# Order of the wide and narrow products inside the feed-forward panels: four orders in turn instead of one

## The chip, the cores and the metric

The kernel runs on one core of a Trainium2 chip. The metric is the device time of one execution in microseconds; three runs of the kernel before gave 3351.51 us (median), 3348.92 us (lowest) and 3356.8 us (highest). Lower is better.

## The reference

Three transformer-like blocks run one after another on 256 tokens of 2048 features, in fp32. Blocks 2 and 3 end in a feed-forward part, and these two parts are what the change touches:

```python
D_MODEL, SEQ, D_FF = 2048, 256, 8192
# block 2, and block 3 with w_up, w_down in place of w_ff1, w_ff2
h = rms_norm(x, g)
x = x + jnp.square(jax.nn.relu(h @ w_ff1)) @ w_ff2      # 2048 -> 8192 -> 2048
```

Everything else (a recurrence, three kinds of attention, gating, pooling) is computed around them by background tasks and stays as it is.

## The kernel before, in words

Every weight product of the kernel runs through one function, `run` (line 180), over a list of `Panel`s. A panel is 512 columns of a weight times an activation of 256 tokens, over `nk` = 16 blocks of 128 rows. The panel is cut into 4 **groups** of 4 row blocks (`kg` = 4), and a group into 4 **units** `j`, one for each 128 output features. Each unit of a panel has a PSUM bank of its own (tags m0 to m3); a unit's sum grows over the four groups.

To keep fp32 accuracy a weight is split in two: `whi` is the rounded part, `wlo` the rest. The activation is stored as (hi | lo) next to each other, 512 columns. So each row block of a unit needs two products: a **wide** one (line 249: `whi` times all 512 columns) and a **narrow** one (line 250: `wlo` times the 256 hi columns, added into the right half of the bank). A unit in a group is thus 4 wide and 4 narrow products, a group 16 pairs, a panel 64 pairs. Each product loads its own 128x128 weights first (PEld in the profile), and the load runs beside the product before.

```python
mm(out, hi[:, c], a, start=st, stop=False, skip_group_check=True)
mm(out[:, 256:512], lo[:, c], a[:, 0:256], start=False, stop=en, skip_group_check=True)
```

While group i is multiplied, the weights of group i+1 are split by `cut`: ScalarE casts `wf` to `whi` (line 209), VectorE subtracts to get `wlo` (line 210), once for each half of a group (two row blocks). `cut` for the first half is written behind unit 0 of group i, for the second half behind unit 1. There are 4 buffers of `whi` and of `wlo`, that is two groups.

After the last group of a panel each unit is taken out of its bank by `sum_halves`: ScalarE copies the right half (line 272), VectorE adds the left half to it (line 275), and the bank is free for the same unit of the next panel. Written order on the engines at the end of a panel is therefore: copy of unit 0, cast of half 0, copy of unit 1, cast of half 1 on ScalarE; `wlo` of half 0, add of unit 0, `wlo` of half 1, add of unit 1 on VectorE. Both engines work strictly in that order. What follows an add differs: in the first product of the feed-forward (an **up** panel) relu, square and a split into `hid` (lines 1101, 1103, 280, 282), in the second (a **down** panel) a multiplication and an addition to `x` on VectorE (lines 1114, 1116).

`ff` (line 1086) writes the panels of a feed-forward part: for each of 4 slices `d` of 2048 hidden features, four up panels `q` = 0 to 3 and four down panels `q` = 0 to 3. That makes 32 panels in each of the two parts, 64 in all, 4096 pairs. The other panels that matter below are those of mode "T" (lines 255 to 257), in which all three products of a row block are 512 wide.

Of the kernel before, what the change touches and what calls it, by code (L numbers as in the profile page):

```python
# [17 lines left out]
# columns of the packed per-feature vectors (each vector of n features takes n / 128 columns)  # L18
# [15 lines left out]
class Panel:  # L34
    """Products of one block of weight columns with an activation held as (hi | lo) tiles.
    w: the weight as it is loaded, [block of columns, unit of rows, 128, rows / 128 * columns]."""

    def __init__(self, w, c0, ncols, nk, act, evac, mode="F", k0=0, pre=None, post=None, load=None):
        self.w, self.c0, self.ncols, self.nk, self.act, self.evac = w, c0, ncols, nk, act, evac
        self.mode, self.k0, self.pre, self.post, self.load = mode, k0, pre, post, load  # L40
        self.kg = min(nk, 2048 // ncols)
        self.ngroups = nk // self.kg
        self.half = self.kg // 2


class FM:
    """A feature-major tensor [128 * n, 256] as tiles of four rows of blocks."""
# [8 lines left out]
class HL:  # L56
    """An activation (hi | lo), two blocks of 128 features to a tile."""
# [8 lines left out]
class Builder:  # L66
# [64 lines left out]
    def step(self, busy=False):  # L131
        """One stage of each task; of the evacuations' later stages only a few, none in a busy slot."""
# [24 lines left out]
    def wait(self, key):  # L157
        """st[key], in a task: other tasks go on until it is there."""
        while key not in self.st:
            yield  # L160
        return self.st[key]

    def wait_tiles(self, *keys, n=4):
        """The n products of each of the keys, in a task."""
        for key in keys:
            for j in range(n):
                yield from self.wait((key, j))

    def get(self, key, f):
        """Block f of the (hi | lo) activation st[key], once it is on its way."""  # L170
        self.require(lambda: key in self.st and f in self.st[key].ready)
        return self.st[key][f]

    def start(self, gen):
        """First stage of what happens to a product; the further ones follow, one a step."""
# [4 lines left out]
    def run(self, panels):  # L180
# [39 lines left out]
        for i, (p, g) in enumerate(groups):  # L220
# [12 lines left out]
            # where, among the units of this group, the next group is split  # L233
            when = (0, 1) if len(units) == 4 else (-1, 0 if len(units) == 2 else -1)
            for u in range(2):
                if when[u] < 0:
                    cut(i + 1, u)
            for j, tag in units:
# [3 lines left out]
                for kk in range(p.kg):  # L242
                    hi, lo = hs[kk // p.half][:, kk % p.half, :], ls[kk // p.half][:, kk % p.half, :]
                    a = p.act(g * p.kg + kk)
                    st = g == 0 and kk == 0
                    en = last and kk == p.kg - 1
                    if p.mode == "F":
                        c = slice(j * 128, (j + 1) * 128)
                        mm(out, hi[:, c], a, start=st, stop=False, skip_group_check=True)  # L249
                        mm(out[:, 256:512], lo[:, c], a[:, 0:256], start=False, stop=en, skip_group_check=True)  # L250
                    else:
                        ah = a[:, j * 128:(j + 1) * 128]
# [5 lines left out]
                self.step(j in when)  # L258
                if last:
                    self.start(p.evac(j, out))  # L260
                if j in when:
                    cut(i + 1, when.index(j))
                if p.mode == "T":
                    self.step()
# [3 lines left out]
    def sum_halves(self, p):  # L268
        """The product of a weight tile: its two halves in PSUM, added."""
# [8 lines left out]
    def split_act(self, dst, src):  # L278
        """dst (hi | lo) of src, both parts exact."""
# [4 lines left out]
    def scaled_split(self, dst, src, g):  # L284
        """dst (hi | lo) of src * g, g one number per partition."""
# [10 lines left out]
    def sum_sq(self, accs):  # L296
        """Sums over partitions and tiles ([128, 256] each), token-major, in PSUM [128, 2]."""
# [15 lines left out]
    def bcast_psum(self, rt):  # L313
        """A token-major [128, 2], over all partitions: [128, 256]."""
# [12 lines left out]
    def attention(self, heads, q, k, v, bias, dim, out):  # L327
        """Softmax attention of query tiles (tokens 0-127 on keys 0-127, 128-255 on 0-255).
        q, k: feature-major [dim, 256]; v(h, t): token-major [128, dim]; bias(h, s, p) is a task that
        writes s [128, 384] = scores + bias; out(i, psum [128, 256])."""  # L330
# [49 lines left out]
    def block1_constants(self):  # L380
# [19 lines left out]
        # 1 - x of mu_r, mu_k, mu_v and of k_a  # L400
# [5 lines left out]
    def input_norm(self, x, gname, hl, key):  # L406
        """hl (hi | lo) of x * g, four blocks at a time, then st[key]: sums of squares."""
# [17 lines left out]
    def load_x(self, name, between=False):  # L425
        """x, feature-major; the later tiles between the first tiles of the weights, or at once."""
# [10 lines left out]
    def block1(self):  # L437
# [36 lines left out]
        # attention, eight heads at a time: q, k feature-major, v token-major  # L474
# [44 lines left out]
        # LoRA: (h + (shift(h) - h) mu) w = h ((1 - mu) w) + shift(h) (mu w)  # L519
# [23 lines left out]
        def mixed(key, n, hf):  # L543
            """y + (shift(y) - y) mu of the product y"""
# [25 lines left out]
        # gated attention branch  # L570
# [70 lines left out]
        # merged branches  # L641
# [59 lines left out]
    def residual(self, hl, gname, key):  # L701
        """x += rms(o) post_norm_g; hl of x * g for what follows; st[key] of 1 / rms(x)."""
# [24 lines left out]
    def rwkv(self, hf):  # L727
        """The recurrence of eight heads, in chunks of 64 tokens."""
# [4 lines left out]
        # decay and in-context rate  # L733
# [16 lines left out]
        # 1 / max(|k k_k|, 1e-12) per head  # L750
# [72 lines left out]
        # (I - L)^-1 per head and chunk: diagonal blocks of 32 by substitution, one block per partition  # L823
# [58 lines left out]
        # the block below the diagonal: X21^T = X11^T L21^T X22^T  # L882
# [19 lines left out]
        # the recurrence over chunks  # L902
# [31 lines left out]
        # par: heads 2i + par; features, and tokens of V, at f; tokens of U at w  # L934
# [53 lines left out]
        # per token and head normalised y stands in v, feature-major  # L988
# [18 lines left out]
    def group_norm(self, y, out, key):  # L1007
        """Per token and head (over 64 values): (y - mean) / sqrt(var + eps), turned feature-major.
        y: PSUM [128, 4, 64], heads 2i on the lower tokens, 2i + 1 on the upper."""
# [27 lines left out]
    def rstd_task(self, key, sums, n, scale=None, square=False):  # L1037
        """st[key] = (token-major, over partitions, over partitions * scale or squared) of 1 / rms."""
# [19 lines left out]
    def acc_sq(self, accs, x, i, n, scale=None, last=1):  # L1058
        """accs, whose sum is the sum of the n tiles (x * scale)^2: the last ones stand by themselves."""
# [26 lines left out]
    def ff(self, w1, w2, h, rkey, done):  # L1086
        """x += relu(norm(x) w1)^2 w2, 2048 hidden features at a time; done(f) when x[f] is whole.
        h is x g: the square of 1 / rms(x), one number a token, comes in after w2."""
# [37 lines left out]
        for d in range(4):  # L1126
            for q in range(4):
                P.append(Panel(w1, 2048 * d + 512 * q, 512, 16, lambda kt: self.get(h, kt), up(d, q)))
            for q in range(4):
                P.append(Panel(w2, 512 * q, 512, 16, lambda kt, d=d: hact(d, kt), down(d, q), k0=16 * d))  # L1130
        return P

# [10 lines left out]
    def block2(self, start):  # L1143
# [20 lines left out]
        # index scores and the 64 keys of each query  # L1164
# [48 lines left out]
        # spatial gating: v token-major  # L1213
# [87 lines left out]
    def topk(self):  # L1301
# [35 lines left out]
        for t in range(2):  # L1337
# [12 lines left out]
            # 0 for a key that is selected and not after its query, else large and negative  # L1350
# [5 lines left out]
    def mixing(self):  # L1356
        """Layer norm of gelu(v) over features, and its causal mix over each 128 tokens."""
# [72 lines left out]
    def two_norms(self):  # L1430
        """x = rms(x) final_g (r1), then the scale of rms of that (r2); st["r3"] is r1 r2."""
# [127 lines left out]
    def pool(self, hf):  # L1559
        """Trailing means minus the value, two groups of 256 channels, mixed within each group."""  # L1560
# [94 lines left out]
def _dilated_bias():  # L1655
    """-slope * distance + ln(number of patterns that hold the key); far below where none does."""
# [8 lines left out]
def _tiles(w, cols=512, rows=256):  # L1665
    """A weight [K, C] in blocks of columns, each in units of rows that stand as they are loaded."""
# [5 lines left out]
def host_layout(i):  # L1672
    """The inputs as the program reads them: slices, transposes and gathers only; and constants
    of the shapes."""
# [46 lines left out]
```

## Time and profile before

| what | value |
|---|---|
| median of three runs | 3351.51 us |
| span of the profiled execution, first to last instruction | 3342.3 us |
| TensorE (PE) busy | 3288.9 us, 98% of the span |
| weight loads (PEld) busy | 2826.5 us, 85% |
| VectorE (DVE) busy | 2066.9 us, 62% |
| ScalarE (ACT) busy | 1716.4 us, 51% |
| share of the DMA engines | about 0.6 in the feed-forward parts |
| feed-forward of block 2, from about | 1604 to 2315 us |
| feed-forward of block 3, from about | 2617 to 3327 us |

The execution that was profiled has no time of its own apart from its span; the median stands 9.2 us above the span, and a change of the span is carried over to the median as it is. Durations of products in the profile overlap (their ends are modelled), so the pace of TensorE is read from the distance of starts, not from the durations.

### The profile page before, as it was taken

To read this page: it belongs to the slowest core of one execution; us is meant where nothing else is said; L and a number is where in the kernel's file an instruction comes from. 1 tells how busy PE (TensorE), PEld (TensorE's weight loads), DVE (VectorE), ACT (ScalarE), POOL (GpSimd) and SP (SyncE) were. 2 spreads that over 40 slices of the span, in tenths; PEclk is the share of its full clock that TensorE was granted. 3 is DMA by queue.
4 is the path that set the end of the run, shared out by engine and by line. 5 is a ranking of instruction groups with operands and counts; after the bars stand their busy time and mean duration, and the time that the engine had idled before them with its cause. 6 is when DMAs were issued, how large, how long until landed. Compare 5 with 4: busy or idle time off the path is not lost.

```text
span 3342.3 us, 50547 instructions
## 1 busy us (share of the span) xinstructions
PE 3288.9 (98%) x19438; PEld 2826.5 (85%) x19438; DVE 2066.9 (62%) x3034; ACT 1716.4 (51%) x2868; POOL 556.2 (17%) x568
## 2 busy tenths in 40 slices
PE   8999999999989999999999999999999999999998
PEld 7787888888878888888888888888888888888887
DVE  5577657646476546576555555658757755565556
ACT  5454544435444574455545545456455654545454
POOL 2132131204130322233100000004224300000001
PEclk9999999999989999999999999999999999999999
DMA  6555535535545555656565556565555556655564
GB/s 205 167 160 162 158 95 170 164 120 188 190 131 172 184 156 183 196 184 187 184 200 189 185 188 196 189 189 184 183 178 166 184 185 188 195 189 189 188 191 145
DMA packets 175585, 589.91 MB, mean 177 GB/s; under 512 B 28784, under 2 KB 31984, under 8 KB 175344
## 3 DMA queue, kind: packets, MB, share of 16 engines
q1 hardware_dynamic: 174624, 585.47, 55.8%
q8 instruction: 152, 2.49, 0.3%
q10 hardware_dynamic: 720, 1.22, 0.1%
q14 instruction: 89, 0.73, 0.1%
HBM read 582.95 MB, written 3.67 MB: 176 GB/s over the span
## 4 chain that ended last, share of the span: by engine, by line
PE 76%; DVE 4%; issue 3%; ACT 2%; POOL 1%; DVEq 0%; POOLq 0%; ACTq 0%
PE pm L249 45%; PE pm L250 23%; DVE wlo L210 2%; PE pm L255 1%; PE pm L257 1%; PE pm L256 1%; ACT whi L209 1%; DVE ev L275 0%; PE ppv L365 0%; POOL ev L661 0%; PE pgr L912 0%; PE psc L338 0%; PE pY L978 0%; PE ppl L1591 0%; DVE mr L1344 0%
## 5 line engine op out<-in xcount | busy, mean ns | idle before, releaser
L210 DVE TENSOR_TENSOR wlo<-wf,whi 128x1024 fp32r<-128x1024 f32 x1086 | 1349.4, 1266 | 1128.6 <-ACT whi L209 1109.2
L249 PE MATMUL pm<-h,whi 128*128 128x512 f32 x3872 | 1376.0, 398 | 12.9 <-ACT whi L209 8.7
L209 ACT CAST whi<-wf 128x1024 fp32r<-128x1024 f32 x1086 | 1107.2, 1050 | 479.8 <-PE pm L249 391.3
L250 PE MATMUL pm<-h,wlo 128*128 128x256 f32 x3872 | 1087.9, 281 | 6.7 <-DVE wlo L210 6.6
L249 PEld LDWEIGHTS pm<-h,whi 128*128 128x128 f32 x3872 | 727.0, 188 | 188.9 <-ACT whi L209 9.0
L250 PEld LDWEIGHTS pm<-h,wlo 128*128 128x128 f32 x3872 | 733.3, 189 | 12.1 <-DVE wlo L210 11.5
L249 PE MATMUL pm<-hid,whi 128*128 128x512 f32 x2048 | 710.8, 391 | 0.0
L250 PE MATMUL pm<-hid,wlo 128*128 128x256 f32 x2048 | 573.3, 280 | 0.0
L272 ACT COPY ev<-pm 128x256 f32<-128x256 f32 x491 | 181.2, 369 | 695.5 <-PE pm L250 679.8
L249 PEld LDWEIGHTS pm<-hid,whi 128*128 128x128 f32 x2048 | 383.1, 187 | 84.6
L249 PE MATMUL pm<-hb,whi 128*128 128x512 f32 x1168 | 421.0, 403 | 11.4 <-DVE hb L717 8.6
L250 PEld LDWEIGHTS pm<-hid,wlo 128*128 128x128 f32 x2048 | 387.0, 189 | 0.0
L1072 POOL TENSOR_TENSOR acc<-acc,sqa 128x256 f32<-128x256 f32 x104 | 120.2, 1162 | 1496.0 <-ACT sqa L1067 1472.5
L250 PE MATMUL pm<-hb,wlo 128*128 128x256 f32 x1168 | 330.1, 283 | 1.3 <-DVE wlo L210 1.1
L249 PEld LDWEIGHTS pm<-hb,whi 128*128 128x128 f32 x1168 | 221.4, 190 | 68.3 <-issue 8.7
L250 PEld LDWEIGHTS pm<-hb,wlo 128*128 128x128 f32 x1168 | 223.4, 191 | 4.2 <-DVE wlo L210 3.1
L275 DVE TENSOR_TENSOR ev<-pm,ev 128x256 f32<-128x256 f32 x491 | 198.9, 416 | 27.0 <-ACT ev L272 26.8
L249 PE MATMUL pm<-mg,whi 128*128 128x512 f32 x512 | 179.6, 395 | 0.0
L250 PE MATMUL pm<-mg,wlo 128*128 128x256 f32 x512 | 143.8, 281 | 1.0 <-DVE wlo L210 1.0
L249 PEld LDWEIGHTS pm<-mg,whi 128*128 128x128 f32 x512 | 96.0, 187 | 22.6
L250 PEld LDWEIGHTS pm<-mg,wlo 128*128 128x128 f32 x512 | 96.7, 189 | 1.7 <-DVE wlo L210 1.6
L255 PE MATMUL pm<-whi,hb 128*128 128x512 f32 x160 | 66.0, 412 | 0.0
(353 smaller groups left out, 3099.9 us busy)
## 6 DMA issues: line engine op xcount, KB each, us to landing
wf<-w_in SPq DMA_DIRECT2D x312, 512.0 KB, 4.0
wf<-w_ff SPq DMA_DIRECT2D x256, 512.0 KB, 4.4
wf<-w_sgu SPq DMA_DIRECT2D x128, 512.0 KB, 3.9
wf<-w_up SPq DMA_DIRECT2D x128, 512.0 KB, 4.4
wf<-w_down SPq DMA_DIRECT2D x128, 512.0 KB, 4.3
wf<-w_out SPq DMA_DIRECT2D x96, 512.0 KB, 4.3
wf<-w_branch_attn SPq DMA_DIRECT2D x16, 512.0 KB, 3.6
wf<-w_branch_rwkv SPq DMA_DIRECT2D x16, 512.0 KB, 4.1
```

What stands on the lines that cost most here:

```text
L209: self.nc.scalar.copy(hi, t)
L210: self.nc.vector.tensor_tensor(lo, t, hi.bitcast(F32), op=ALU.subtract)
L249: mm(out, hi[:, c], a, start=st, stop=False, skip_group_check=True)
L250: mm(out[:, 256:512], lo[:, c], a[:, 0:256], start=False, stop=en, skip_group_check=True)
L255: mm(o, ah, hi, start=st, stop=False, skip_group_check=True)
L256: mm(o, ah, lo, start=False, stop=False, skip_group_check=True)
L257: mm(o, al, hi, start=False, stop=en, skip_group_check=True)
L272: nc.scalar.copy(a, p[:, 256:512])
L275: nc.vector.tensor_tensor(b, p[:, 0:256], a, op=ALU.add)
L1072: nc.gpsimd.tensor_tensor(accs[0], accs[0], s, op=ALU.add)
```

## The change

Each panel gets an `order`, 0 to 3, and `ff` gives panel `q` the order `q`, for up and down panels alike. All other panels keep order 0, which is the order before: wide, narrow, wide, narrow. Order 1 takes two row blocks at a time: two wide, then two narrow products. Order 2 takes the whole group: four wide, then four narrow. Order 3 takes two units together: for each row block the wide product of unit j-1 and of unit j, then the narrow ones of both; evacuation and `cut` of both units come behind the second. The rest of the diff removes comments and docstrings, which moves line numbers (209 becomes 210, 249 becomes 247 in "F" mode, 275 becomes 310).

```diff
+            def products(j, half):
+                ...
+                    if kind == "h":
+                        mm(out, hs[kk // p.half][:, kk % p.half, c], a, start=g == 0 and kk == 0, stop=False,
+                           skip_group_check=True)
+                    else:
+                        mm(out[:, 256:512], ls[kk // p.half][:, kk % p.half, c], a[:, 0:256], start=False,
+                           stop=last and kk == p.kg - 1, skip_group_check=True)
+
+            def after(j):
+                self.step(j in when)
+                if last:
+                    self.start(p.evac(j, ps[j]))
+                if j in when:
+                    cut(i + 1, when.index(j))
...
+                    if p.order == 3 and len(units) == 4:
+                        if j % 2 == 0:
+                            if g == 0:
+                                ps[j + 1] = self.pm.tile([128, 512], F32, name="pm", tag=units[j + 1][1])
+                            continue
+                        for kk in ks:
+                            for kind in "hl":
+                                for jj in (j - 1, j):
+                                    products(jj, [(kind, kk)])
+                        after(j - 1)
+                        after(j)
+                        continue
+                    if p.order == 1:
+                        seq = [(kind, kk + d) for kk in range(0, p.kg, 2) for kind in "hl" for d in range(2)]
+                    elif p.order == 2:
+                        seq = [(kind, kk) for kind in "hl" for kk in ks]
                     else:
+                        seq = [(kind, kk) for kk in ks for kind in "hl"]
+                    products(j, seq)
...
-                P.append(Panel(w1, 2048 * d + 512 * q, 512, 16, lambda kt: self.get(h, kt), up(d, q)))
+                P.append(Panel(w1, 2048 * d + 512 * q, 512, 16, lambda kt: self.get(h, kt), up(d, q), order=q))
...
-                P.append(Panel(w2, 512 * q, 512, 16, lambda kt, d=d: hact(d, kt), down(d, q), k0=16 * d))
+                P.append(Panel(w2, 512 * q, 512, 16, lambda kt, d=d: hact(d, kt), down(d, q), k0=16 * d, order=q))
```

**On TensorE, the start of up panel 3 (order 3) in slice d = 0 of block 2's part.** `pm_15990` is the bank of unit 0; the bank of unit 1 is `pm_16005` before and `pm_15992` now; `pm_15817` is the bank of the panel before. Before:

```order
L250 MATMUL pm_15817<-h2_15305,wlo_15903 128x256
L249 MATMUL pm_15990<-h2_14620,whi_15937 128x512
L250 MATMUL pm_15990<-h2_14620,wlo_15938 128x256
...
L250 MATMUL pm_15990<-h2_14652,wlo_15954 128x256
L249 MATMUL pm_16005<-h2_14620,whi_15937 128x512
L250 MATMUL pm_16005<-h2_14620,wlo_15938 128x256
```

and now:

```order
L250 MATMUL pm_15817<-h2_15305,wlo_15903 128x256 x2
L247 MATMUL pm_15990<-h2_14620,whi_15937 128x512
L247 MATMUL pm_15992<-h2_14620,whi_15937 128x512
L250 MATMUL pm_15990<-h2_14620,wlo_15938 128x256
L250 MATMUL pm_15992<-h2_14620,wlo_15938 128x256
...
L247 MATMUL pm_15990<-h2_14652,whi_15953 128x512
L247 MATMUL pm_15992<-h2_14652,whi_15953 128x512
```

The first product into the bank of unit 1 stood ninth in the panel and stands second now.

**On TensorE, a unit of up panel 2 (order 2) in the same slice.** `pm_15776` is the bank of its unit 0, `pm_15791` that of unit 1; x2 are two row blocks from one buffer. Before:

```order
L249 MATMUL pm_15776<-h2_14620,whi_15723 128x512
L250 MATMUL pm_15776<-h2_14620,wlo_15724 128x256
...
L249 MATMUL pm_15776<-h2_14652,whi_15739 128x512
L250 MATMUL pm_15776<-h2_14652,wlo_15740 128x256
...
L249 MATMUL pm_15791<-h2_14620,whi_15723 128x512
L250 MATMUL pm_15791<-h2_14620,wlo_15724 128x256
```

and now:

```order
L247 MATMUL pm_15776<-h2_14620,whi_15723 128x512 x2
L247 MATMUL pm_15776<-h2_14652,whi_15739 128x512 x2
L250 MATMUL pm_15776<-h2_14620,wlo_15724 128x256 x2
L250 MATMUL pm_15776<-h2_14652,wlo_15740 128x256 x2
L247 MATMUL pm_15791<-h2_14620,whi_15723 128x512 x2
```

Where wide and narrow products alternated there are now four wide ones in a row and then four narrow ones.

**On VectorE, the end of up panel 3 and the start of down panel 0.** `pm_15990` and the three names behind it are the banks of units 0 to 3. Before:

```order
L210 TENSOR_TENSOR wlo_16152<-wf_16046,whi_16151 128x1024
L275 TENSOR_TENSOR ev2_16163<-pm_15990,ev_16149 128x256
L210 TENSOR_TENSOR wlo_16168<-wf_16092,whi_16167 128x1024
L275 TENSOR_TENSOR ev2_16180<-pm_16005,ev_16165 128x256
L275 TENSOR_TENSOR ev2_16196<-pm_16018,ev_16183 128x256
```

and now:

```order
L211 TENSOR_TENSOR wlo_16162<-wf_16048,whi_16161 128x1024
L310 TENSOR_TENSOR ev2_16165<-pm_15990,ev_16159 128x256
L211 TENSOR_TENSOR wlo_16170<-wf_16094,whi_16169 128x1024
L310 TENSOR_TENSOR ev2_16190<-pm_15992,ev_16167 128x256
L310 TENSOR_TENSOR ev2_16198<-pm_16019,ev_16193 128x256
```

Nothing moved here: apart from names and line numbers VectorE, ScalarE, GpSimd and the DMA queue keep their order in the whole program. What moved is when TensorE ends units 0 and 1, for which the copies ahead of these adds wait.

## Rows read from the trace of the kernel before

**Rows 1.** The page's head, and its part 1: busy time of each engine

```profile
span 3342.3 us, 50547 instructions
PE 3288.9 (98%) x19438; PEld 2826.5 (85%) x19438; DVE 2066.9 (62%) x3034; ACT 1716.4 (51%) x2868; POOL 556.2 (17%) x568
```

**Rows 2.** Windows, both feed-forward parts: length, busy by engine, PEclk, DMA share, GB/s

```profile
1605.00:2315.00 710.00, 710.00 (x4100) 625.52 (x4099) 422.81 (x584) 378.81 (x619) 30.59 (x26) 1.00 0.60 189
2618.00:3327.00 709.00, 709.00 (x4095) 624.95 (x4094) 415.34 (x580) 373.62 (x608) 25.13 (x22) 1.00 0.59 185
```

**Rows 3.** Timeline (start, us, engine, line): a down panel's start, the next one's

```profile
2048.10 0.19 PEld L249 LDWEIGHTS pm<-hid,whi 128*128 128x128 f32 x1
2048.21 0.39 PE L249 MATMUL pm<-hid,whi 128*128 128x512 f32 x1
...
2070.40 0.39 PE L249 MATMUL pm<-hid,whi 128*128 128x512 f32 x1
```

**Rows 4.** Timeline, a panel of mode "T": line 255's products, 27 starts apart

```profile
2499.74 0.39 PE L255 MATMUL pm<-whi,h 128*128 128x512 f32 x1
...
2505.86 0.39 PE L255 MATMUL pm<-whi,h 128*128 128x512 f32 x1
```

**Rows 5.** Weight loads: eight behind one-column products (timeline), all of line 250 (page)

```profile
3330.44 0.97 PEld L301 LDWEIGHTS pst<-ones,sqa 128*128 128x128 f32 x8
...
L250 PEld LDWEIGHTS pm<-hid,wlo 128*128 128x128 f32 x2048 | 387.0, 189 | 0.0
```

**Rows 6.** Timeline of ACT, end of an up panel (the next starts at 2048.21)

```profile
2044.25 0.37 ACT L272 COPY ev<-pm 128x256 f32<-128x256 f32 x1 [5.74 <-PE pm L250]
2044.52 1.05 ACT L209 CAST whi<-wf 128x1024 fp32r<-128x1024 f32 x1
2045.64 0.37 ACT L272 COPY ev<-pm 128x256 f32<-128x256 f32 x1
2045.91 1.05 ACT L209 CAST whi<-wf 128x1024 fp32r<-128x1024 f32 x1
```

**Rows 7.** Timeline of DVE, the same stretch

```profile
2045.60 1.23 DVE L210 TENSOR_TENSOR wlo<-wf,whi 128x1024 fp32r<-128x1024 f32 x1 [5.65 <-ACT whi L209]
2046.74 0.42 DVE L275 TENSOR_TENSOR ev<-pm,ev 128x256 f32<-128x256 f32 x1
2047.08 1.22 DVE L210 TENSOR_TENSOR wlo<-wf,whi 128x1024 fp32r<-128x1024 f32 x1
2048.21 0.75 DVE L275 TENSOR_TENSOR ev<-pm,ev 128x256 f32<-128x256 f32 x2
```

**Rows 8.** Timeline, end of a down panel: the next panel's first product, and DVE

```profile
2136.96 0.39 PE L249 MATMUL pm<-h,whi 128*128 128x512 f32 x1
...
2136.96 0.42 DVE L1114 TENSOR_TENSOR ev<-ev,rq 128x256 f32<-128x256 f32 x1
2137.30 0.42 DVE L275 TENSOR_TENSOR ev<-pm,ev 128x256 f32<-128x256 f32 x1
```

**Rows 9.** Timeline, block 2's part, last d, down panel 3: start, a wait for an add

```profile
2292.34 0.39 PE L249 MATMUL pm<-hid,whi 128*128 128x512 f32 x1
...
2293.22 0.41 DVE L275 TENSOR_TENSOR ev<-pm,ev 128x256 f32<-128x256 f32 x1
...
2293.61 0.28 PE L250 MATMUL pm<-hid,wlo 128*128 128x256 f32 x1
2293.69 0.19 PEld L249 LDWEIGHTS pm<-hid,whi 128*128 128x128 f32 x1
```

**Rows 10.** Timeline, block 3's first product behind it, and the add of unit 1

```profile
2314.97 0.40 PE L249 MATMUL pm<-h,whi 128*128 128x512 f32 x1
...
2315.77 0.41 DVE L275 TENSOR_TENSOR ev<-pm,ev 128x256 f32<-128x256 f32 x1
```

**Rows 11.** Timeline of DVE, the program's last panel: last unit's add, last step into x

```profile
3327.89 0.42 DVE L275 TENSOR_TENSOR ev<-pm,ev 128x256 f32<-128x256 f32 x1 [0.22 <-ACT ev L272]
...
3329.02 0.42 DVE L1116 TENSOR_TENSOR x<-x,ev 128x256 f32<-128x256 f32 x1
```

More of the change, by code (lines that the diff above doesn't have):

```diff
@@ L34, with __init__ @@
 class Panel:
-    def __init__(self, w, c0, ncols, nk, act, evac, mode="F", k0=0, pre=None, post=None, load=None):
+    def __init__(self, w, c0, ncols, nk, act, evac, mode="F", k0=0, pre=None, post=None, load=None, order=0):
+        self.order = order
         self.w, self.c0, self.ncols, self.nk, self.act, self.evac = w, c0, ncols, nk, act, evac
@@ L237, in run @@
                     cut(i + 1, u)
+            def products(j, half):
+                out = ps[j]
+                c = slice(j * 128, (j + 1) * 128)
+                for kk in half:
+                    kind, kk = kk
+                    a = p.act(g * p.kg + kk)
+                    if kind == "h":
[10 more added lines that the diff above has]
+                    cut(i + 1, when.index(j))
+                if p.mode == "T":
+                    self.step()
             for j, tag in units:
@@ L241, in run @@
                 out = ps[j]
[L242 to L250, printed above, removed]
-                    else:
+                if p.mode == "F":
+                    ks = range(p.kg)
+                    if p.order == 3 and len(units) == 4:
[14 more added lines that the diff above has]
+                        seq = [(kind, kk) for kind in "hl" for kk in ks]
+                    else:
+                        seq = [(kind, kk) for kk in ks for kind in "hl"]
+                    products(j, seq)
+                else:
+                    for kk in range(p.kg):
+                        hi, lo = hs[kk // p.half][:, kk % p.half, :], ls[kk // p.half][:, kk % p.half, :]
+                        a = p.act(g * p.kg + kk)
+                        st = g == 0 and kk == 0
+                        en = last and kk == p.kg - 1
                         ah = a[:, j * 128:(j + 1) * 128]
@@ L257, in run @@
                         mm(o, al, hi, start=False, stop=en, skip_group_check=True)
[L258 to L264, printed above, removed]
+                after(j)
             if last and p.post:
```

## The prediction

> **What bounds the kernel now.** I read the page's head and engine shares first, then the windows of the two feed-forward parts, then the timeline at panel borders. TensorE is busy for 98% of the span [rows 1]. In both feed-forward parts it has no idle time at all, at the full granted clock, 2.4 GHz, while ScalarE and VectorE are busy for 53% to 60% and the DMA engines for 60% [rows 2]. Busy time hides small gaps, so the pace is what counts: a panel, 64 pairs, takes 2070.40 - 2048.21 = 22.19 us from first product to first product [rows 3], or 346.7 ns a pair. 768 columns at 2.4 GHz are 320 ns; so a pair pays 26.7 ns beyond its columns. Products of 512 columns only, in mode "T", stand 6.12 us / 27 = 226.7 ns apart, 13.3 ns beyond their columns [rows 4]. Both fit one sentence: every product costs its columns plus 13.3 ns (a wide one 226.7, a narrow one 120), and its weight load is hidden behind the product before.
>
> Two things follow. There is no stall in these parts for a new order to remove; 32 panels of 22.19 us are the 710 us of a part. And the change can act only through the pace, or by putting waits where there are none.
>
> **The change part by part: the pace.** No product, load, cast, add or DMA is added or removed; 48 panels (3072 pairs) change their order on TensorE alone. By the sentence above a sum of columns plus a constant doesn't depend on the order: 0 us. A load has to fit behind the product ahead of it, and a load starts when that product starts: the first load of a panel stands at 2048.10 and its product at 2048.21, 0.11 us later [rows 3]. A narrow product gives it 0.12 us whether a wide or a narrow one follows, and there are as many loads behind narrow products as before. What the trace doesn't show is narrow after narrow. There are now 512 + 768 + 512 = 1792 such places (2, 3 and 2 for each 4 pairs in orders 1, 2 and 3, with 1024 pairs each). Bounds from the nearest rows: the 13.3 ns could vanish there, as low as 106.7 ns, -24 us in all; or the load, recorded with 189 ns [rows 5], could show, +69 ns each, +124 us. Eight loads in a row behind one-column products end within 0.97 us, (0.97 - 0.19) / 7 = 0.11 us apart [rows 5], so a load fits, and wide after wide keeps its 13.3 ns [rows 4]; I take 0.
>
> **The waits that order 1 and 2 add: none.** A panel's units still end at the same times. The second half of a group is needed no earlier than now but for `whi` in order 2, 0.45 us behind a group's start where 0.69 us was; its cast ends at 2045.91 + 1.05 = 2046.96, 1.25 us ahead of the start [rows 6]. Buffers come free within half a microsecond of before. Cost 0.
>
> **Order 3 at its start.** Unit 1's first product moves from 1.39 us behind the panel's start to the second place, and its load to the start itself. It needs bank m1, which is free when VectorE has added unit 1 of the panel before. After an up panel that add runs from the new panel's start, 2048.21, for 0.42 us [rows 7]. From an add's end to the load that waits for it the trace has 2293.22 + 0.41 to 2293.69, 0.06 us [rows 9]. TensorE works in order, so all behind it waits: 0.48 us, in 8 up panels 3: 3.8 us. After a down panel a multiplication stands ahead of that add, which ends at 2137.72, 0.76 us behind the start [rows 8]: 0.82 us, in 7 panels: 5.7 us. In block 2's last slice VectorE also makes the next block's activation; there the add ends 1.29 us behind the start at 2292.34 [rows 9]: 1.35 us. Together 10.9 us.
>
> **Order 3 at its end.** Units 0 and 1 of the last group now end together, 8 pairs (2.77 us) ahead of the border, where unit 0 ended 12 pairs (4.16 us) ahead. Behind unit 0's copy are queued, on ScalarE, both casts for the next panel, and on VectorE both `wlo` and the adds. From the border, before: copy 0 at -3.96, that is 0.20 behind its unit's end [rows 6]; `wlo` of half 0 at -2.61, add 0 at -1.47, `wlo` of half 1 from -1.13 to +0.09 [rows 7]. This is a chain without gaps but for that end (copy to cast 0.27, cast to `wlo` 1.08, `wlo` to add 1.14, add to `wlo` 0.34); copy 1 and cast 1 run beside it in both cases. So all of it comes 1.39 us later: add 0 ends at +0.34, `wlo` of half 1 at +1.48.
> The next panel has order 0. Its first load stands at -0.11 and waits for bank m0 until 0.34 + 0.06 = +0.40: 0.51 us. The narrow product of its third row block has its load at +0.69 (2 pairs) and waits for the second `wlo` until 1.54: 0.85 us in all, which contains the 0.51. Unit 1's load at +1.28 waits for add 1: after an up panel until 1.40 + 0.42 + 0.06 = 1.88, which 0.85 covers; after a down panel, with the multiplication of 0.34 ahead, until 2.22, that is 0.94 in all.
> Up 3 to down 0: 8 x 0.85 = 6.8 us. Down 3 to up 0: 6 x 0.94 = 5.6 us. Block 2's last panel to block 3: the add of unit 1 stands at 2315.77, 0.80 behind the border [rows 10]; 1.39 later it ends at 2.60, + 0.06 against 1.28: 1.4 us. Together 13.8 us. A border's lateness is not handed on: the next casts come 1.4 us later than now but TensorE is 0.85 later too, and ScalarE and VectorE, 40% and more of their time free [rows 2], have a group of 5.55 us to catch up in.
>
> **The end of the program.** The last panel has order 3 too. Units 2 and 3 end together with it, and VectorE's queue from add 2 on (add 2, x, multiplication, add 3, x, multiplication, x) starts when unit 3's add starts now, 3327.89: six steps of 0.34 us put the last step at 3329.93 against 3329.02 [rows 11]: 0.9 us.
>
> **Sum.** 0 + 10.9 + 13.8 + 0.9 = 25.6 us more. On the span 3342.3 that is 3367.9; on the median, 9.2 us above it, 3377.1 us, 0.77% slower. What a measurement of this kernel can tell from no change is about 0.2%, 6.7 us.
>
> **The rivals.** *Runs of narrow products are cheaper* (not slower): if the 13.3 ns belongs to the change of width, or a narrow product can start at once when a narrow one is ahead, the 1792 places give back up to 24 us, and the time is 25.6 - 23.9 = 1.7 us above now, 3353 us. From 10.5 ns a place on it brings the sum within 6.7 us of no change; below that the waits win. For it: nothing in the trace has narrow after narrow in this type. Against it: wide after wide, without a change of width, pays in full [rows 4].
> The Trainium skill, page "TensorE: Matmul & The Clock Gate", section "Back-to-back issue gap", gives columns / 2.4 + 2.5 ns for warm products that follow each other. By it, as an estimate, narrow after narrow would be 109 ns, the saving 1792 x 11 = 19 us and the sum near 3358 us. By the same rule wide after wide would be 216 ns; the trace has 226.7 [rows 4], so the rule doesn't hold for this type of product, and I give it little.
> *Order 3 also sheds it by changing banks* (faster): if the 13.3 ns is paid for going on in the same bank, all 2048 products of order 3 shed it, 27 us, and with narrow runs of orders 1 and 2 (1280 x 13.3 = 17 us) the time would be 3351.5 + 25.6 - 27 - 17 = 3333 us. Against it: line 255 to 257's products stay in one bank for a whole unit and a feed-forward panel changes banks 16 times, yet 64 x (226.7 + 106.7 + 13.3) is 22.19 us to the last digit [rows 3, 4]; free changes would have left 21.97.
> *Loads show behind narrow runs* (slower): 189 ns as recorded instead of 120 gives up to 3377 + 124 = 3501 us; 10 ns give 3395. Against it: the 0.11 us of [rows 5], and of every narrow-to-wide step now.
> That the change doesn't do what it says is excluded by TensorE's order at the places shown above.
>
> **How the numbers follow.** Forecast (waits, pace as now) 0.80; narrow runs cheaper in full 0.10; bank change as well 0.03; loads show 0.07. Predicted time 3377 us. Range: below, half of the narrow runs' saving, 12 us, gives 3365; above, 0.17 us more at each of 31 waits (a load that has to run again in full, 0.11, and one more hand-over) adds 5, and the highest run of before stood 5.3 above its median: 3388. Both rivals with 0.07 and 0.10 lie outside. Faster 0.03, within 0.2% 0.10, slower 0.87.
>
> **What would show it.** Right: in the profile after, TensorE's weight loads wait for VectorE, 15 times for `wlo` and some 38 times for an add (16 into order 3, 15 for bank m0 and 7 for m1 out of it), 0.1 to 1.4 us each, all at borders into and out of order 3; panels of order 1 and 2 last 22.19 us. Wrong: a panel of order 2 that is shorter or longer than 22.19 us (the pace was wrong), or borders without waits (the chains were).

## The result and the profile after

The changed kernel takes 3385.16 us (median of four runs, 3373.61 to 3389.51), the kernel before 3350.22 us beside it; the ratio on record is 1.0091, 95% interval 1.0067 to 1.0114 (that of the two medians alone is 1.0104). The prediction was 3377 us, 3365 to 3388. The change is slower by about the amount forecast, but, as the rest shows, partly for another reason.

The page after, head and part 1, as [rows 1], and the windows of the two feed-forward parts, as [rows 2], cut at their first and last products:

```profile
span 3387.8 us, 50571 instructions
PE 3323.6 (98%) x19438; PEld 2833.5 (84%) x19438; DVE 2069.2 (61%) x3034; ACT 1715.5 (51%) x2868; POOL 549.8 (16%) x568
```

```profile
1615.02:2341.63 726.61, 722.40 (x4110) 626.62 (x4108) 422.93 (x585) 378.35 (x618) 32.62 (x27) 1.00 0.59 186
2642.45:3370.49 728.04, 723.80 (x4109) 626.61 (x4108) 419.26 (x583) 376.15 (x612) 25.67 (x25) 1.00 0.58 182
```

The count of products and loads is as before, and TensorE still shows 98%. In [rows 2] its busy time filled the parts; now 4.2 us of each are idle. But the parts are 15 us longer each, so most of the loss is not idle time in this view: either products started later while the one ahead is shown as running, or the pace fell. Only distances of starts tell it.

**The span misleads.** It is 45.5 us longer than in [rows 1], the medians differ by 35. 11.9 us of the 45.5 lie ahead of block 2's feed-forward part (first product at 1615.02 instead of 1603.12), where neither code nor order changed. The window of the first 1000 us, of before and of after (the third number from the end is the granted clock):

```profile
8.00:1000.00 992.00, 965.39 (x6257) 799.50 (x6258) 625.27 (x983) 479.23 (x811) 236.69 (x244) 0.99 0.51 158
```

```profile
8.00:1000.00 992.00, 965.13 (x6209) 799.53 (x6210) 619.55 (x972) 473.20 (x799) 236.70 (x244) 0.98 0.50 157
```

The same 992 us hold 48 products fewer, at a lower granted clock: stretches at 1.2 GHz, the lower level, last 27 us in all before and 48 us after. Ahead of one such stretch of before, at 943 us, TensorE had waited 0.98 and 1.06 us for an activation. The experiments show that the time in them changes from one execution to the next with the same kernel.

**The waits that came.** The waits view of both kernels (engine, tile and line, what it waited for: us in total, times, longest), before and after; line 249 became 247, 275 became 310:

```profile
PEld pm L250 <- DVE wlo L210: 23.1, 34, 1.6
...
PEld pm L249 <- DVE ev L275: 11.0, 13, 1.8
...
PE pm L249 <- DVE ev L275: 7.8, 12, 1.5
```

```profile
PEld pm L250 <- DVE wlo L211: 25.4, 50, 1.5
...
PE pm L247 <- DVE ev L310: 16.3, 36, 1.6
...
PEld pm L247 <- DVE ev L310: 14.5, 20, 1.9
```

There are 16 more waits for `wlo` (15 forecast) and 31 more for an add (about 38 forecast), so they are where the prediction put them. Their shape, at the start of a down panel of order 3 (timeline of after; the panel starts at 2136.47, as [rows 8] at 2136.96):

```profile
2136.36 0.19 PEld L247 LDWEIGHTS pm<-hid,whi 128*128 128x128 f32 x1
...
2136.47 0.39 PE L247 MATMUL pm<-hid,whi 128*128 128x512 f32 x1
...
2136.76 0.42 DVE L310 TENSOR_TENSOR ev<-pm,ev 128x256 f32<-128x256 f32 x1
...
2137.29 0.19 PEld L247 LDWEIGHTS pm<-hid,whi 128*128 128x128 f32 x1 [0.74 <-ACT ev L307]
2137.32 0.47 PE L247 MATMUL pm<-hid,whi 128*128 128x512 f32 x1 [0.46 <-DVE ev L310]
...
2137.63 0.40 PE L250 MATMUL pm<-hid,wlo 128*128 128x256 f32 x2
```

The load of unit 1 stands 0.82 us behind the panel's start, as forecast (the add ends 0.05 earlier, the load follows it 0.05 later). But its product stands only 0.03 behind the load. A wide product ahead ends its turn after 0.23, so the product is 0.85 - 0.23 = 0.62 late, and the next distance (0.31 instead of 0.23) adds 0.08: 0.69 in all, not 0.82.

**The pace.** First products of seven panels in a row in after (three up panels, q = 1 to 3, and four down panels, q = 0 to 3) and of the one behind:

```profile
2001.51 0.40 PE L247 MATMUL pm<-h,whi 128*128 128x512 f32 x1
...
2023.82 0.40 PE L247 MATMUL pm<-h,whi 128*128 128x512 f32 x1
...
2046.28 0.39 PE L247 MATMUL pm<-h,whi 128*128 128x512 f32 x1
...
2069.30 0.47 PE L247 MATMUL pm<-hid,whi 128*128 128x512 f32 x1 [0.20 <-DVE ev L310]
...
2091.72 0.39 PE L247 MATMUL pm<-hid,whi 128*128 128x512 f32 x1
...
2114.02 0.40 PE L247 MATMUL pm<-hid,whi 128*128 128x512 f32 x1
...
2136.47 0.39 PE L247 MATMUL pm<-hid,whi 128*128 128x512 f32 x1
...
2159.83 0.47 PE L247 MATMUL pm<-h,whi 128*128 128x512 f32 x1 [0.20 <-DVE ev L310]
```

Against the 22.19 us of [rows 3]: order 1 takes 22.31 and 22.30, order 2 takes 22.46 and 22.45, with no wait in them; order 3 takes 23.02 (up) and 23.36 (down), waits included; and order 0, which didn't change, takes 22.42 here with a wait at its start, but 22.81 in the seven other slices.

### The profile page after: what moved, and what is told of

Its sections match the earlier page's. It is cut to its first block, busy times and chain, and to the rows that moved or that the text cites. A ratio compares the mean times of both kernels' runs of the same rounds, so it can differ in the third digit from the quotient of the medians.

```text
span 3387.8 us, 50571 instructions
## 1 busy us (share of the span) xinstructions
PE 3323.6 (98%) x19438; PEld 2833.5 (84%) x19438; DVE 2069.2 (61%) x3034; ACT 1715.5 (51%) x2868; POOL 549.8 (16%) x568
## 4 chain that ended last, share of the span: by engine, by line
PE 87%; DVE 5%; issue 4%; ACT 2%; POOL 1%; DMA 0%; DVEq 0%; POOLq 0%; ACTq 0%
PE pm L247 51%; PE pm L250 25%; DVE wlo L211 3%; PE pm L296 2%; PE pm L298 2%; PE pm L297 2%; ACT whi L210 2%; DVE ev L310 1%; PE pgr L947 1%; PE ppv L400 1%; PE psc L373 0%; PE pY L1013 0%; PE pY L1016 0%; PE psc L372 0%; POOL ev L696 0%
## 5 line engine op out<-in xcount | busy, mean ns | idle before, releaser
L247 PE MATMUL pm<-h,whi 128*128 128x512 f32 x3872 | 1312.9, 401 | 16.5 <-ACT whi L210 8.4
L250 PE MATMUL pm<-h,wlo 128*128 128x256 f32 x3872 | 942.7, 281 | 5.5 <-DVE wlo L211 5.3
L247 PEld LDWEIGHTS pm<-h,whi 128*128 128x128 f32 x3872 | 686.0, 189 | 148.1 <-issue 10.4
L250 PEld LDWEIGHTS pm<-h,wlo 128*128 128x128 f32 x3872 | 715.7, 189 | 68.2 <-DVE wlo L211 11.6
L247 PE MATMUL pm<-hid,whi 128*128 128x512 f32 x2048 | 644.6, 396 | 5.7 <-DVE ev L310 5.7
L250 PE MATMUL pm<-hid,wlo 128*128 128x256 f32 x2048 | 427.2, 280 | 0.0
L250 PEld LDWEIGHTS pm<-hid,wlo 128*128 128x128 f32 x2048 | 367.7, 188 | 57.6 <-DVE wlo L211 1.5
L247 PEld LDWEIGHTS pm<-hid,whi 128*128 128x128 f32 x2048 | 340.1, 188 | 44.4 <-ACT ev L307 6.5
L310 DVE TENSOR_TENSOR ev<-pm,ev 128x256 f32<-128x256 f32 x491 | 198.9, 416 | 28.6 <-ACT ev L307 28.4
```

What stands on the lines that cost most here:

```text
L247: mm(out, hs[kk // p.half][:, kk % p.half, c], a, start=g == 0 and kk == 0, stop=False, skip_group_check=True)
L250: mm(out[:, 256:512], ls[kk // p.half][:, kk % p.half, c], a[:, 0:256], start=False, stop=last and kk == p.kg - 1, skip_group_check=True)
L310: nc.vector.tensor_tensor(b, p[:, 0:256], a, op=ALU.add)
```

## The experiments

In the table the third column sums the 64 panels of a trace against the first trace of before (711.85 + 712.73 us); the fourth is the start of block 2's part, the fifth the time at 1.2 GHz in the first 1000 us.

| kernel | ratio to before | two parts, us | block 2's part from | 1.2 GHz, us | what it is |
|---|---|---|---|---|---|
| r_before | 0.9997 [0.9988, 1.0007] | 0.0 | 1612.4 | 44.4 | before, again |
| one2 | 1.0001 [0.9990, 1.0011] | +2.1 | 1605.8 | 27.3 | order 2 in 16 groups |
| all2 | 1.0040 [1.0028, 1.0052] | +16.2 | 1608.0 | 37.5 | order 2 everywhere |
| mid3 | 1.0044 [1.0021, 1.0067] | +14.3 | 1616.0 | 58.0 | order 3 in middle groups |
| only12 | 1.0045 [1.0029, 1.0060] | +11.4 | 1603.0 | 30.7 | orders 0, 1, 2, 0 |
| first3 | 1.0056 [1.0043, 1.0069] | +18.0 | 1602.8 | 23.9 | order 3, last group order 0 |
| ord1 | 1.0076 [1.0060, 1.0092] | +26.5 | 1611.1 | 47.8 | orders 1, 1, 2, 3 |
| r_after | 1.0103 [1.0085, 1.0121] | +28.6 | 1613.6 | 58.0 | after, again |
| only3 | 1.0104 [1.0081, 1.0127] | +30.6 | 1608.4 | 44.4 | orders 0, 0, 0, 3 |
| after | 1.0091 [1.0067, 1.0114] | +30.7 | 1615.0 | 47.8 | the change |

The letters of theories belong to the text in which they stand.

**r_after and r_before: the same kernels again.** No edit.

> The changed kernel once more. Its first profile was 45.5 us longer than that of before: 14.9 us in the feed-forward of block 2, 15.4 us in that of block 3, 11.9 us ahead of the first of them, where no instruction is moved, 3.3 us elsewhere. Theory A: the feed-forward parts cost about 30 us again (waits at the borders of order 3 about 19 us, slower pace about 12 us); what lies ahead of them varies from run to run with the stretches of low granted clock and is not of the change, so some runs of this kernel stand only 25 to 30 us above before. Theory B: the loss ahead of the feed-forward parts belongs to the change, and the first product of block 2's feed-forward stands near 1615 us in every profile of this kernel, against 1603 before.

> The kernel before once more, for a second trace. Theory A (the stretches of half granted clock ahead of block 2's feed-forward part vary from execution to execution, whatever the kernel): block 2's part starts anywhere between 1603 and 1616 us, later with more time at half clock, and the two feed-forward parts last the same as in the first trace, 711.7 and 712.6 us, with panels of 22.19 us wherever TensorE has no wait. Theory B (the changed kernel itself causes the later start): the part starts at 1603 again with about 27 us at half clock in the first 1000 us. Ratio 1.000 by both.

r_after: 3380.66 us (3377.01 to 3388.31). r_before: 3350.19 us (3345.94 to 3356.26), with panels of 22.19 us in the quiet stretches and its feed-forward part 9.3 us later than in the first trace of before. With no edit, the start moved by most of the 11.9 us; and only12 and first3, which hold most of the change, start at 1603 like the first trace. So the later start isn't of the change. The window of the first 1000 us of mid3, with the lowest granted clock, for comparison with the two above:

```profile
8.00:1000.00 992.00, 965.84 (x6200) 801.46 (x6201) 618.90 (x971) 472.96 (x799) 235.75 (x244) 0.97 0.50 156
```

Taken over 66 single runs, each with its mean granted clock, and each kernel against its own mean, the time rises by 0.83 us for each microsecond of (1 - clock) x time. At equal clock after and r_after stand 31.7 and 30.1 us above r_before, all2 15.5, first3 18.3, ord1 27.3: nearly the third column of the table, which is read inside the two parts alone. That column is thus nearly all that the change costs; what lies outside the two parts stands under "The sum" below.

**only3: order 3 without orders 1 and 2; only12: orders 1 and 2 without order 3.** Edits, in both panel lists:

```diff
-  order=q))
+  order=(0, 0, 0, 3)[q]))      only3
+  order=(0, 1, 2, 0)[q]))      only12
```

> Order 3 in panels q = 3, order 0 in all others. Theory A: the waits at the borders stay, about 19 us, and the pace of order 3 costs 0.11 us a panel, 1.8 us; order 0 behind a wait may run in its slower rhythm, 353 ns a pair instead of 347, 0.43 us a panel, in up to 48 panels: +21 to +41 us on before. If the prediction's account were whole (waits alone, no change of pace), +25.6 us with every panel of order 0 at 22.19 us away from the borders.

> Orders 1 and 2 in panels q = 1 and 2, order 0 in q = 0 and q = 3: no two units together, so no new wait. Theory A: panels of order 1 last 22.30 us and of order 2 22.45 us, 6.0 us in all, and the panels of order 0 behind them run in either rhythm, 0 to 0.43 us each in 32 panels: +6 to +20 us. The prediction's account (order costs no pace): 0 us. The rival with cheap runs of narrow products: about -17 us.

only12 has the waits of before, but for one more for `wlo`, and none at its quiet borders; and yet the parts are 11.4 us longer, which can't be without a change of pace. Its panels, down q = 0 to 3 and the up panel behind, then up q = 3 of the next slice and the panel behind it:

```profile
2051.64 0.39 PE L247 MATMUL pm<-hid,whi 128*128 128x512 f32 x1
...
2073.82 0.39 PE L247 MATMUL pm<-hid,whi 128*128 128x512 f32 x1
...
2096.12 0.40 PE L247 MATMUL pm<-hid,whi 128*128 128x512 f32 x1
...
2118.58 0.40 PE L247 MATMUL pm<-hid,whi 128*128 128x512 f32 x1
...
2141.19 0.40 PE L247 MATMUL pm<-h,whi 128*128 128x512 f32 x1
...
2163.81 0.40 PE L247 MATMUL pm<-h,whi 128*128 128x512 f32 x1
...
2208.54 0.40 PE L247 MATMUL pm<-h,whi 128*128 128x512 f32 x1
...
2230.73 0.39 PE L247 MATMUL pm<-hid,whi 128*128 128x512 f32 x1
```

Order 0 takes 22.18, order 1 22.30, order 2 22.46, and then order 0, unchanged, 22.61 and 22.62: 353 ns a pair for a whole panel, without a wait, where it was 346.7. It is a second, slower rhythm of the old order; the difference is all in the wide product, 236.7 ns from its start to the next one instead of 230.0, with 116.7 for the narrow one in both. Up q = 3, behind orders 1 and 2 like down q = 3, is back at 22.19. only3 keeps the waits, and its parts are as long as in the full change: the orders 1 and 2 that it lacks cost 6 us there, but 16 of its 32 panels q = 1 and 2, all of order 0, run in the slow rhythm (22.62 us, the other quiet ones 22.19). Taking the orders out one by one doesn't add up, since the slow rhythm fills the gap.

**mid3 and first3: the waits of order 3, both away, and the start alone.** Edits:

```diff
-  if p.order == 3 and len(units) == 4:
+  if p.order == 3 and len(units) == 4 and 0 < g < p.ngroups - 1:      mid3
+  if p.order == 3 and len(units) == 4 and g < p.ngroups - 1:          first3
```

> As the change, but panels q = 3 take order 3 in their two middle groups alone and order 0 in the first and the last, so that the banks and the copies at the borders come as before. Theory A: the waits, about 19 us of the change, are gone, and the weight loads wait for no add at the borders; what is left is pace, 6.0 us for orders 1 and 2, 0.9 us for order 3, and up to 0.43 us for each panel of order 0: +7 to +17 us. If the waits were not the cause, about as slow as the change, +30 us or more.

> Order 3 in all groups of its panels but the last, which has order 0; orders 1 and 2 as in the changed kernel. Theory A (start and end of order 3 wait apart from each other): the waits at the start stay (first gap about 0.5 us in up panels, 0.85 in down panels, 1.4 in block 2's last slice: 9 us in all), those at the end go, so the two feed-forward parts last about 1439 + 9 = 1448 us together (1439 is the kernel whose first and last groups both have order 0; 1454 to 1455 the changed kernel). Theory D (the lateness at the start is only what the end of the panel before left, or the reverse: the two are one wait): the waits go on both sides, 1439, or stay on both, 1454.

The waits views, mid3 and then first3:

```profile
PEld pm L250 <- DVE wlo L211: 22.4, 34, 1.6
...
PEld pm L247 <- DVE ev L310: 10.9, 12, 1.8
...
PE pm L247 <- DVE ev L310: 7.8, 12, 1.5
```

```profile
PEld pm L250 <- DVE wlo L211: 23.3, 34, 1.6
...
PE pm L247 <- DVE ev L310: 12.2, 20, 1.5
...
PEld pm L247 <- DVE ev L310: 11.7, 15, 1.8
```

mid3 has the counts of before, but for one; first3 shows 11 more for adds than mid3 and as many for `wlo`. Start and end are two separate things, as forecast: those of the start remain in first3 (first distances 0.52 us in up panels, 0.86 in down panels, 1.40 in block 2's last slice), those of the end are gone. The forecast for first3 was 1448 us for both parts, it took 1442.6: in mid3 every panel q = 0 but block 2's first runs in the slow rhythm (22.62 in quiet ones), in first3 four of sixteen. The waits at the start cost what was expected; that order 0 ran in its fast rhythm more often was not foreseen.

**all2 and one2: order 2 everywhere, and in 16 single groups.** Edits:

```diff
-  order=q))
+  order=2))                                     all2
+  order=(0, 0, 2, 0)[q]))                       one2
-  elif p.order == 2:
+  elif p.order == 2 and g == 0:                 one2
```

> All 64 feed-forward panels have order 2; no panel has another order beside it. Theory A (an order has a pace of its own, and the slow rhythm belongs to order 0): every panel lasts 22.45 us, +0.26 each, the two parts together 16.6 us longer than before, none at 22.6, no wait at a border; ratio about 1.005. Theory C (what costs is the passage from one order to another, and a panel that follows one): all panels 22.19 us, the parts as before, ratio 1.000. The prediction's sum of columns plus a constant also says 1.000.

> Order 0 everywhere, but for the first of the four groups of panel q = 2, which has order 2: 16 of 256 groups. Theory A1 (order 0 has two rhythms, 346.7 and 353.3 ns a pair, and which one runs is set by what went ahead and then lasts): behind such a group panels of order 0 go on at 22.6 us instead of 22.19, at least behind down panel 2, until a wait or another such group sets them again; the two parts get longer by between 5 and 25 us, far more than the groups themselves cost (16 x 0.065 = 1 us). Theory A2 (the time belongs to the reordered products alone): 1 us, ratio 1.000, all other panels at 22.19 us.

all2 settles that an order has a pace: three starts in a row,

```profile
2058.40 0.40 PE L247 MATMUL pm<-hid,whi 128*128 128x512 f32 x1
...
2080.86 0.40 PE L247 MATMUL pm<-hid,whi 128*128 128x512 f32 x1
...
2103.31 0.40 PE L247 MATMUL pm<-hid,whi 128*128 128x512 f32 x1
```

22.45 us in every quiet panel, 16.2 us in all (16.6 expected), none in a slow rhythm, none at 22.19. From start to start a wide product takes 232.3 ns and a narrow one 118.5 (means of 1280 each), against 230.0 and 116.7 before. one2 went against the theory of a rhythm set by any such group: a panel with one group of order 2 takes 22.25 us (+0.06), the panels behind it 22.19, and 2.1 us in all are left; the slow rhythm came up in four panels only, the first of each part (block 3's first has it in r_before, too) and the last two of block 2's part, behind a short wait. So one group of another order, without a wait, doesn't bring it.

**allwide: every product 512 wide.** The narrow products, too, take all columns (they add the term of `wlo` and the lo half):

```diff
+  elif p.order == 4:
+      mm(out, ls[kk // p.half][:, kk % p.half, c], a, start=False, stop=last and kk == p.kg - 1, ...)
-  order=q))
+  order=4))
```

> In the 64 feed-forward panels the wlo products too take all 512 columns (they add wlo times the lo half, which is left out before), in the alternating order; so every product is wide and follows a wide one with another weight. Theory E (in these panels, with the weight as stationary operand, a wide product behind a wide one costs more than mode T's 226.7 ns): 232 to 236 ns from start to start, a panel of 128 products 29.7 to 30.2 us. Theory F (the 226.7 ns of mode T hold here too, and the 233 ns of the changed kernel come from the mix of widths): 226.7 ns, a panel 29.0 us, as the prediction's sentence also has it. The two parts together are 437 us longer by F and 480 to 512 us by E, since 4096 narrow products become wide.

Its products, `whi` and `wlo` in turn, and the distance of two panels (of two later starts):

```profile
2039.76 0.39 PE L247 MATMUL pm<-hid,whi 128*128 128x512 f32 x1
2039.99 0.39 PE L250 MATMUL pm<-hid,wlo 128*128 128x512 f32 x1
2040.22 0.39 PE L247 MATMUL pm<-hid,whi 128*128 128x512 f32 x1
2040.44 0.39 PE L250 MATMUL pm<-hid,wlo 128*128 128x512 f32 x1
...
2186.64 0.39 PE L247 MATMUL pm<-hid,whi 128*128 128x512 f32 x1
...
2215.66 0.39 PE L247 MATMUL pm<-hid,whi 128*128 128x512 f32 x1
```

29.01 us for 128 products, 226.7 ns each, the figure of mode "T" [rows 4] (3785.43 us, 433 above before, where 437 were expected by this figure; ratio 1.1292, 1.1268 to 1.1316). So a wide product behind a wide one isn't dearer in these panels; the 233 ns that it takes in orders 1 to 3 come from the mix of widths.

**ord1: order 1 in place of order 0.** Edit: `order=(1, 1, 2, 3)[q]`.

> Panels q = 0 have order 1 in place of order 0; q = 1 to 3 as in the changed kernel (1, 2, 3). Theory G (the slow rhythm, 353.3 ns a pair, belongs to order 0): panels q = 0 last 22.30 us and the waits behind order 3 (0.4 to 0.6), so 22.5 to 22.9, none more; the two feed-forward parts are 27 us longer than before instead of 28.6 to 30.7 (5 for the slow rhythm go, 1.75 for order 1 come). Theory H (whatever follows order 3 is slowed): panels q = 0 stay at 22.8 to 23.0 and the parts 29 to 31 us longer. The prediction's pace of 0 would have q = 0 at 22.19 and the waits.

Starts of up q = 3 and down q = 0, 1 and 2:

```profile
2041.47 0.39 PE L247 MATMUL pm<-h,whi 128*128 128x512 f32 x1
...
2064.49 0.47 PE L247 MATMUL pm<-hid,whi 128*128 128x512 f32 x1 [0.20 <-DVE ev L310]
...
2086.88 0.40 PE L247 MATMUL pm<-hid,whi 128*128 128x512 f32 x1
...
2109.17 0.40 PE L247 MATMUL pm<-hid,whi 128*128 128x512 f32 x1
```

The panel behind order 3 takes 22.39 (after an up panel) or 22.7 (after a down panel), wait included, never 22.8 to 23.0. The parts are 26.5 us longer, 27 expected. The slow rhythm belongs to the alternating order.

## Why the prediction was right in size and wrong in part

**What bounds the kernel: right.** TensorE's pace and waits alone made the difference; the queues of the other engines kept their order, and their busy time stayed within 0.2% (VectorE 2069.2 us against 2066.9, ScalarE 1715.5 against 1716.4).

**Pace 0: wrong, and the largest miss.** In after it costs about 12 us: order 1 1.75 (16 panels), order 2 4.2, order 3 1.7 apart from its waits, and 4.6 for panels of order 0 that fell into the slow rhythm (2.7 in r_after). The step that failed is "a sum of columns plus a constant doesn't depend on the order". The sentence was taken from two regular sequences, alternating and all wide, and it holds for both (346.7 and, in allwide, 226.7); for runs of two or four it is short by 1.6 and 4.2 ns a pair (22.30 and 22.45 us by 64). The prediction looked for the risk at narrow after narrow and bounded it from both sides, but it called wide after wide settled. It also took one pace for the old order, though its own rows hold a second one: block 2's last down panel lasts 2314.97 - 2292.34 = 22.63 us [rows 9, 10], 0.07 of the 0.44 above 22.19 a wait and the rest pairs of 353 ns.

**The rivals about narrow runs fell.** Narrow products take 118.5 ns in order 2 and 115.2 in orders 1 and 3 (116.7 in alternation), where 120 was taken for one, and the wide ones got slower by more: 1792 places give back nothing near 24 us. The loads don't show behind them. Order 3's changes of bank shed nothing. By the Trainium skill, page "TensorE: Matmul & The Clock Gate", section "Back-to-back issue gap", narrow after narrow would have been 109 ns and wide after wide 216. The page gives this as the gap of a single product, with no budget for weight loads, while here each product loads its own. The runs have 118.5 in order 2 and, in allwide, 226.7, so the rule was rightly given little weight.

**Orders 1 and 2 add no waits: right.** only12 has none at its quiet borders. But "panels of order 1 and 2 last 22.19 us", which the prediction named as its own test, failed at 22.30 and 22.45.

**Order 3 at its start: 10.9 forecast, 9.0 measured.** Place, cause and count held (16 adds, and block 2's last slice the longest). Each border was over by 0.12 to 0.13: 0.36 instead of 0.48 (up), 0.69 instead of 0.82 (down), 1.23 instead of 1.35. The lateness of the load was taken for that of its product. A load that waits is hidden no more, but the product follows it in 0.03 us instead of 0.23, and most of that is won back.

**Order 3 at its end: 13.8 forecast, about 11 measured.** Read where order 0 runs in its fast rhythm, a border from up to down costs 0.59 (0.85 forecast): 0.36 at the border and 0.23 inside the next panel, which takes 22.42. One from down to up costs 0.79 (0.94 forecast): 0.36 and 0.43, in panels of 22.62. Into block 3 it is about 1.3 (1.4). The chain ran a little earlier than derived: the border would have been at 2159.48 without the wait (0.35 ahead of 2159.83), add 0 ended at 2159.69, 0.21 behind it (0.34 forecast), the second `wlo` at 2160.82, 1.34 behind (1.48 forecast):

```profile
2159.27 0.42 DVE L310 TENSOR_TENSOR ev<-pm,ev 128x256 f32<-128x256 f32 x1
...
2159.60 1.22 DVE L211 TENSOR_TENSOR wlo<-wf,whi 128x1024 fp32r<-128x1024 f32 x1
2159.80 0.19 PEld L247 LDWEIGHTS pm<-h,whi 128*128 128x128 f32 x1 [0.37 <-issue]
...
2160.87 0.19 PEld L250 LDWEIGHTS pm<-h,wlo 128*128 128x128 f32 x1 [0.20 <-DVE wlo L211]
2160.87 0.39 PE L250 MATMUL pm<-h,wlo 128*128 128x256 f32 x1
```

Here, too, load and product start together at 2160.87, which saves 0.11 more. The waits come to about 20 us where 24.7 were forecast.

**The end of the program: right.** From the last product to the last step into `x`, 2.27 us in the trace of before and 3.22 in after: 0.95, 0.9 forecast. Another 1.2 us came behind it, up to the last instruction (14.05 us against 12.82). There the granted clock falls to 1.2 GHz, in after 2.9 us and in before 5.4 us behind the start of the last weight product. That isn't of the change: over the twelve traces these last steps take 14.0 us in the five where the clock fell within 2.9 us, and 12.8 to 13.0 in the seven where it fell after 4.0 us or more, r_after among them (4.9 us; 13.03).

**The sum.** 25.6 forecast; read in the trace, 30.7 in the parts, 0.7 more between them and 0.95 at the end, 32; by medians 30 to 35. Waits too large by 5 and a pace too small by 12 partly cancelled, so the median came 8 us above the forecast and inside the range; that it did is in part luck. What made the span of after look worse still, 12 us ahead of the changed code, is the granted clock of that one execution.

**Open.** What sends order 0 into the slow rhythm isn't settled. It isn't the change's own: block 2's last down panel has it in before, 22.63 us, and not in r_before, 22.28 us, the same kernel. Where no wait comes between, a panel of order 1 and one of order 2 turned the rhythm over: in only12 fast into slow (7 of 7, all in down panels) and slow into fast (6 of 6, all in up panels), in mid3 slow into fast (13 of 13, up and down). So in these passages the rhythm ahead decides, and not the kind of panel. Behind the middle groups of order 3 the slow rhythm came each time (mid3, 16 of 16), one of them out of the slow one. One group of order 2 leaves the fast rhythm as it is (one2). Behind waits either comes, even where they are equal to 0.01 us (after, r_after). Why a run of wide products among narrow ones is dearer than in a row without any isn't settled either.

## What to carry over

A pace that was measured in two regular sequences doesn't hold for a third one: an order of products that the trace doesn't show deserves a bound on each kind of step in it, the familiar ones too. When a bank or an operand is asked for earlier, what counts is when its producer's queue gets there; and the delay of a product is read from the distance of starts, since the late load of its weights is followed at once by its product. Before a difference of two spans is explained, compare a stretch that the change doesn't touch; here it differed by 12 us.

## What the hardware showed that I had not expected

- One and the same instruction sequence, wide and narrow in turn, runs at 346.7 or at about 353.4 ns a pair for a whole panel (22.19 or 22.62 us), without any wait shown, and stays in either over panel borders; the kernel before shows both. Whole panels of orders 1 and 2 between turned one into the other, 26 times of 26.
- Runs of two or four in a mix of widths cost more than alternation in its fast rhythm and less than in its slow one: 350.8 ns a pair in order 2 (232.3 for the wide product, 118.5 for the narrow one), 346.7 in the fast rhythm (230.0 and 116.7), 353.4 in the slow one (236.7 and 116.7). Where all products are wide, one takes 226.7.
- The time at 1.2 GHz in the unchanged first 1000 us varied from 24 to 58 us among eleven traces (the table and the first of before), and with it the start of the next part from 1602.8 to 1616.0 us.
